# Query-key products of two heads, and the two low-rank products, issued in direct succession on the two row halves of the array

## The chip, the cores and the metric

The kernel runs on one core of one Trainium2 chip. The metric is device time in microseconds (us) of one execution. The kernel before takes 2220.48 us, the median of 3 runs (2214.12 to 2221.47). The engines are TensorE (PE in the profile; its weight loads are listed apart as PEld), VectorE (DVE), ScalarE (ACT), GpSimd (POOL) and SyncE (SP), which here issues most of the weight DMAs.

## The reference

Two transformer blocks over 512 tokens with model width 1024, in float32. The first block has a gated linear recurrence (hgrn2) beside a differential attention, and then a mixture of 32 experts, of which each token takes two. The second has an RWKV-7 mixer beside an attention over selected keys, a cross attention to 256 memory rows, and again 32 experts. Cut to what the change touches:

```python
def diff_attention(q1, q2, k1, k2, v, lam):      # 4 heads, q and k of 64, v of 128
    ...
        def probs(qb, kk):                       # a block of 128 queries
            s = jnp.einsum('bqhd,bshd->bhqs', qb, kk).astype(jnp.float32) * scale
            return jax.nn.softmax(jnp.where(mask, s, -jnp.inf), axis=-1)
        a = probs(qb1, k1) - lam * probs(qb2, k2)
        return jnp.einsum('bhqs,bshv->bqhv', a.astype(v.dtype), v)
...
    w = -jax.nn.softplus(-(w0 + jnp.tanh(xw) @ w2).astype(f32)) - 0.5     # rwkv7_branch, xw of 64
    decay = jnp.exp(-jnp.exp(w))
    a = jax.nn.sigmoid(a0 + xa @ a2)                                      # xa of 64
...
        s = jnp.einsum('bhqr,bqkr->bhqk', ql, c_sel).astype(f32)          # dsa_branch, 8 heads of 64
        s = jnp.where(valid[:, None], s, -jnp.inf)
        p = jax.nn.softmax(s, axis=-1).astype(c_sel.dtype)
```

All three have products that are contracted over 64 numbers, and there are always two of them that belong together: the two softmaxes of one head of the differential attention, the decay and the gate `a` of the low-rank products, and two of the eight heads of the selected attention.

## The kernel before

Activations lie in SBUF; the weights stream in. A dense layer multiplies a high and a low part of each operand (`split`, lines 193 to 196: ScalarE rounds the high part, VectorE subtracts it) in three products (`mm3`, line 198), each of which is an instruction of line 210 with a contraction over all 128 rows of the array. The other products are plain float32 and take two passes: one instruction leaves two matmul records in the trace.

A tensor whose two heads lie in partitions 0 to 63 and 64 to 127 gives two products over 64 rows each, one on the lower and one on the upper half of the array's rows. There are three such places:

- **Differential attention** (`dense1`, lines 541 to 573). For each of 4 heads and 4 blocks of 128 queries: for each of the two softmaxes the query-key product (line 551) into bank a0 or a1, the causal mask, added by a bf16 product (line 552), the maximum of the row (line 553, VectorE), the exponential with its sum (line 556, ScalarE). Then the two are combined on VectorE, transposed on TensorE (line 565) and copied; after four blocks the product with the values follows (line 569). A step with block i has n = 128, 256, 384 or 512 keys. The scheduler has the dense products of the same stage (banks d0 to d3) and those of the recurrence (lines 640 to 670) to put between.
- **Low-rank products** (`dense2`, lines 1295 to 1304). For each of 4 head pairs the decay's product (line 1298) and that of `a` (line 1302), each with a tanh on ScalarE behind it. Then VectorE has a scan and several products over 128 x 512.
- **Selected attention** (`dense2`, lines 1644 to 1676). For each of 4 head pairs p and 4 blocks i: the two query-key products (line 1655) into two of the three banks d0, d1 and a2 in turn, then per head the mask (line 1658), the row maximum (line 1660), a factor (line 1661), the exponential with its sum (line 1663), reciprocal and scaling (lines 1664 and 1665), i + 1 transposes (line 1668) and a copy (line 1669); then for both heads the products with the values (line 1674). After the fourth block the output of the pair is copied into `qT` (line 1676).

Behind the selected attention in the text stand products that do not depend on it: two gates and the RWKV branch's output projection, in the form `dense256` (lines 392 to 406, two banks a0 and a1). The attention's own output projection is the first thing to use `qT`: it is split on ScalarE and VectorE (`yb`, tile GG), and `dense` multiplies it (`ps_d<-GG,wh`).

The order of the work on each engine is not that of the text. A scheduler goes through the program with modelled times and puts ready instructions into each engine's queue, those of earlier lines first; `high_priority` raises a block. `keep_in_program_order` ties an instruction to its place in the text relative to the others that are so tied. On the chip an engine then works off its queue; semaphores make it wait for what it needs.

Of the kernel before, what the change touches and what calls it, by code (L numbers as in the profile page):

```python
# [29 lines left out]
AF = mybir.ActivationFunctionType  # L30
# [148 lines left out]
class Net:  # L179
# [28 lines left out]

    def mm(self, *a, **k):
        self.pin(self.nc.tensor.matmul(*a, **k))  # L210

    def persistent(self):
        tc, nc, es = self.tc, self.nc, self.es
# [195 lines left out]
    def dense1(self, rings, late):  # L409
        tc, nc, I = self.tc, self.nc, self.I  # L410
# [15 lines left out]
        o, n = self.at["cols2"]["norm_mem_2"]  # L426
        self.nmem = A.tile([128, 8], F32, name="nmem")
        nc.gpsimd.dma_start(self.nmem, I["cols2"][:, o:o + n])
        n = sum(v[1] for v in self.at["cols1"].values())
# [31 lines left out]
        o, n = self.at["cols1"]["hg_lb0"]  # L461
# [4 lines left out]
        for k in range(8):  # L466
            b = self.bank("a", (128, 256))
# [42 lines left out]
        qkT = big("C", (128, 2, 4, 512))  # L510
# [8 lines left out]
        for t in range(4):  # L519
            nv = raw[:, t, :].rearrange("p (i h d) -> p i h d", i=2, h=8)  # L520
            nc.vector.tensor_mul(nv, nv, rr[:, t][:, :, :, None].broadcast_to([128, 2, 8, 64]))
            a = k4([128, 2, 8, 64])
            bt = k4([128, 2, 8, 64])
            for i in range(2):
                nc.vector.tensor_mul(a[:, i], nv[:, i], cc[:, t, i][:, None, :].broadcast_to([128, 8, 64]))
                for s in range(2):
                    d0 = slice(s * 32, s * 32 + 32)
                    d1 = slice(32 - s * 32, 64 - s * 32)
# [3 lines left out]
            for i in range(2):  # L532
                b = self.bank("a")
# [6 lines left out]
        for h in range(4):  # L540
            vh = dv[:, :, h * 128:(h + 1) * 128]
            aT = B.tile([128, 4, 512], F32, name="aT", bufs=2)
            for i in range(4):
                n = (i + 1) * 128
                qs = slice(i * 128, n)
                st = wk.tile([128, 8], F32, name="da_st", bufs=4)
                ps = []
                for m in range(2):
                    r = slice(m * 64, (m + 1) * 64)
                    b = self.bank("a%d" % m)  # L550
                    nc.tensor.matmul(b[:, :n], qkT[r, 0, h, qs], qkT[r, 1, h, :n], start=True, stop=False)
                    nc.tensor.matmul(b[:, qs], idb, dgn, start=False, stop=True)
                    nc.vector.reduce_max(st[:, m:m + 1], b[:, :n], axis=AX.X)
                    nc.vector.tensor_scalar(st[:, 2 + m:3 + m], st[:, m:m + 1], -0.125, None, op0=ALU.mult)
                    pe = k3([128, 512])
                    nc.scalar.activation(pe[:, :n], b[:, :n], AF.Exp, scale=0.125, bias=st[:, 2 + m:3 + m],
                                         accum_out=st[:, 4 + m:5 + m])
                    ps.append(pe)
                nc.vector.reciprocal(st[:, 6:8], st[:, 4:6])
                nc.vector.tensor_scalar(ps[1][:, :n], ps[1][:, :n], st[:, 7:8], nlam, op0=ALU.mult, op1=ALU.mult)  # L560
                nc.vector.scalar_tensor_tensor(ps[0][:, :n], ps[0][:, :n], st[:, 6:7], ps[1][:, :n],
                                               op0=ALU.mult, op1=ALU.add)
                b = self.bank("a2")
                for j in range(i + 1):
                    nc.tensor.transpose(b[:, j * 128:(j + 1) * 128], ps[0][:, j * 128:(j + 1) * 128], ident)
                nc.scalar.activation(aT[:, :i + 1, qs], b[:, :n].rearrange("p (j q) -> p j q", q=128), AF.Copy)
            b = self.bank("a2")
            for j in range(4):
                nc.tensor.matmul(b[:, j * 128:], vh[:, j, :], aT[:, j, j * 128:], start=(j == 0), stop=(j == 3))
            nc.scalar.activation(vh, b.rearrange("p (j n) -> p j n", j=4), AF.Copy)  # L570
# [3 lines left out]
        r = A.tile([128, 4, 8], F32, name="onr", bufs=2)  # L574
        b = self.bank("a", (128, 4, 8))
# [6 lines left out]
        for h in range(4):  # L582
            b = self.tok_spread(r, 2 * h, 1)
            o = k3([128, 512])
# [5 lines left out]
        th = big("D")  # L590
# [47 lines left out]
        for m in range(4):  # L638
            tok = slice(m * 128, (m + 1) * 128)
            b = self.bank("a", (128, 4, 64))  # L640
# [6 lines left out]
            b = self.bank("a", (128, 4, 128))  # L647
# [4 lines left out]
            for p in range(2):  # L652
                r = slice(p * 64, (p + 1) * 64)
# [551 lines left out]
    def dense2(self):  # L1205
        tc, nc, I = self.tc, self.nc, self.I
# [9 lines left out]
        n = sum(v[1] for v in self.at["cols2"].values())  # L1216
# [15 lines left out]
        lora = big("lora", (128, 512))  # L1232
# [7 lines left out]
        omu, hw0, ha0, oka, hbg, hka = cc[:, 0:14], cc[:, 14:18], cc[:, 18:22], cc[:, 22:26], cc[:, 26:42], cc[:, 42:46]  # L1240
# [19 lines left out]
        xw = big("xw", (128, 512))  # L1260
# [33 lines left out]
        reset = self.reset(k3([128, 512]))  # L1294
        for p in range(4):
            pc = slice(p * 128, (p + 1) * 128)
            b = self.bank("a")
            nc.tensor.matmul(b, lora[0:64, pc], xw[0:64], start=True, stop=True)
            ld = tmp[:, p, 0]
            nc.scalar.activation(ld, b, AF.Tanh, scale=0.5, bias=hw0[:, p:p + 1])  # L1300
            b = self.bank("a")
            nc.tensor.matmul(b, lora[64:128, pc], xw[64:128], start=True, stop=True)
            th = tmp[:, p, 1]
            nc.scalar.activation(th, b, AF.Tanh, scale=0.5, bias=ha0[:, p:p + 1])
            nc.gpsimd.tensor_scalar(ld, ld, hc, hc, op0=ALU.mult, op1=ALU.add)
            cum = k2([128, 512])
            nc.vector.tensor_tensor_scan(cum, reset, ld, 0.0, op0=ALU.mult, op1=ALU.add)
            nc.vector.tensor_sub(ld, cum, ld)
            nc.scalar.activation(ld, ld, AF.Exp)
            nc.scalar.activation(AR[:, p, :, 1, :], v4(cum), AF.Exp)  # L1310
            nc.scalar.activation(cum, cum, AF.Exp, scale=-1.0)
            b = self.tok_spread(hs, 2 * p, 2)
            kkn = AR[:, p, :, 0, :]
            nc.vector.scalar_tensor_tensor(kkn, v4(kr[:, p, :]), col("rw_k_k_2")[:, p:p + 1], v4(b),
                                           op0=ALU.mult, op1=ALU.mult)
            nc.vector.scalar_tensor_tensor(bx[:, p], v5(th), 1.0, kkn.rearrange("p (m u) n -> p m u n", u=2),
                                           op0=ALU.add, op1=ALU.mult)
            nc.vector.scalar_tensor_tensor(kkn, kkn, -2.0, v4(ld), op0=ALU.mult, op1=ALU.mult)
            nc.gpsimd.tensor_mul(bx[:, p], bx[:, p], v5(cum))
            nc.vector.tensor_scalar(th, th, hka[:, p:p + 1], oka[:, p:p + 1], op0=ALU.mult, op1=ALU.add)  # L1320
            nc.vector.tensor_mul(kr[:, p, :], th, kr[:, p, :])
            nc.vector.tensor_mul(kx[:, p], v5(kr[:, p, :]), v5(cum))
# [51 lines left out]
        for p in range(4):  # L1374
            pc = slice(p * 128, (p + 1) * 128)
# [4 lines left out]
            b = self.bank("a", (128, 4, 128))  # L1380
# [265 lines left out]
        for p in range(4):  # L1646
            bo_ = self.bank("d3")
            for i in range(4):
                n = (i + 1) * 128
                qs = slice(i * 128, n)  # L1650
                sb = []
                for e in range(2):
                    r = slice(e * 64, e * 64 + 64)
                    b = self.bank(("d0", "d1", "a2")[(turn + e) % 3])
                    nc.tensor.matmul(b[:, :n], qT[r, p, qs], KT[r, p, :n], start=True, stop=False)
                    sb.append(b)
                for e, b in enumerate(sb):
                    nc.tensor.matmul(b[:, :n], idb, dgn if i == 0 else bias[:, bo[i]:bo[i] + n], start=False, stop=True)
                    st = wk.tile([128, 4], F32, name="st", bufs=4)
# [218 lines left out]
```

## Time and profile before

| | before |
|---|---|
| median of 3 runs | 2220.48 us |
| the profiled execution | 2217.94 us |
| its span, first to last instruction | 2216.1 us |
| mean granted TensorE clock | 0.976 |
| TensorE busy | 2134.3 us, 96% |
| TensorE's weight loads | 1376.3 us, 62% |
| VectorE busy | 989.7 us, 45% |
| ScalarE busy | 679.0 us, 31% |
| GpSimd busy | 161.1 us, 7% |

Shares are means over the whole span; stages differ. Loads overlap products on TensorE, so its two rows do not add up. Ends of products are modelled: where one starts before the one ahead has ended, the distance from start to start is what it costs. A granted clock of 1.00 is 2.4 GHz, 0.50 is 1.2 GHz.

### The profile page before, as it was taken

What the parts mean: (1) busy time and instruction counts of PE and PEld (TensorE: products, weight loads), DVE (VectorE), ACT (ScalarE), POOL (GpSimd) and SP (SyncE); (2) the same over time, 40 slices, a digit from 0 to 9 for tenths busy, and PEclk for the clock granted to TensorE, in tenths of its full rate; (3) what the DMA queues carried; (4) which work ended last, traced back from release to release, by engine and by line L of the source; (5) the groups of instructions that cost most, each with busy time, mean ns of one, the idle gap of its engine ahead of it and who ended that gap; (6) DMA issues with size and microseconds to landing.
All of it is one profiled execution on the core that took longest, in us unless ns stands there. A gap on an engine that the chain in (4) does not pass through costs nothing. (4 is left out here: it accounts for less than half of the span.)

```text
span 2216.1 us, 30270 instructions
## 1 busy us (share of the span) xinstructions
PE 2134.3 (96%) x12176; PEld 1376.3 (62%) x12176; DVE 989.7 (45%) x1998; ACT 679.0 (31%) x1313; POOL 161.1 (7%) x138
## 2 busy tenths in 40 slices
PE   8999999999999999998998999999898999999996
PEld 7766778785544744445766776667777544444443
DVE  4675323552323523334278485445455133333334
ACT  5364323232111321113533433443443211111113
POOL 0420001200000000000151100002110000000000
PEclk9999899999999999999998999999999999999998
DMA  4221121368999789994222112112624899999994
GB/s 176 84 67 48 48 105 66 141 275 342 401 419 420 300 341 418 420 420 145 84 67 75 60 45 86 38 58 86 254 77 172 338 377 418 419 419 420 420 420 165
DMA packets 95743, 505.89 MB, mean 228 GB/s; under 512 B 21024, under 2 KB 26144, under 8 KB 43888
## 3 DMA queue, kind: packets, MB, share of 16 engines
q1 hardware_dynamic: 90992, 490.09, 55.7%
q10 hardware_dynamic: 4112, 11.66, 1.4%
q8 instruction: 98, 1.61, 0.3%
q0 software_dynamic: 496, 2.17, 0.3%
q14 instruction: 45, 0.37, 0.1%
HBM read 494.83 MB, written 8.91 MB: 227 GB/s over the span
## 5 line engine op out<-in xcount | busy, mean ns | idle before, releaser
L210 PE MATMUL ps_d<-wslot,xg 128*64 128x512 f32 x2048 | 446.6, 593 | 2.4 <-DMA wslot<-in_wm_dram 2.4
L210 PE MATMUL ps_d<-hT,wh 128*128 128x512 f32 x1056 | 348.8, 415 | 2.5 <-DVE hT L301 2.5
L210 PEld LDWEIGHTS ps_d<-wslot,xg 128*64 128x64 f32 x2048 | 148.1, 137 | 289.0 <-issue 275.2
L196 DVE TENSOR_TENSOR wl<-wslot,wh 128x512 fp32r<-128x512 f32 x236 | 170.8, 729 | 286.1 <-ACT wh L195 233.7
L195 ACT ACTIVATE wh<-wslot 128x512 fp32r<-128x512 f32 x260 | 162.7, 630 | 321.9 <-PE ps_d L210 248.5
L210 PEld LDWEIGHTS ps_d<-hT,wh 128*128 128x128 f32 x1056 | 200.2, 196 | 55.6 <-issue 9.3
L210 PE MATMUL ps_d<-hT,wl 128*128 128x512 f32 x528 | 210.9, 411 | 0.5 <-DVE wl L196 0.5
L940 DVE TENSOR_TENSOR s<-ps_d,s 128x512 f32<-128x512 f32 x32 | 22.1, 692 | 420.7 <-PE ps_d L210 420.7
L210 PE MATMUL ps_a<-wslot,hidT 128*64 128x512 f32 (+1 forms) x800 | 173.1, 582 | 2.5 <-ACT hidT L948 2.1
L210 PE MATMUL ps_d<-wh,hT 128*128 128x512 f32 x512 | 165.4, 400 | 2.2 <-ACT wh L195 1.1
L978 DVE TENSOR_TENSOR acc<-acc,ps_a 128x512 f32<-128x512 f32 (+1 forms) x215 | 132.1, 667 | 50.7 <-PE ps_a L210 50.6
L210 PE MATMUL ps_a<-yy,S 128*128 128x512 f32 (+1 forms) x454 | 121.6, 397 | 8.7 <-DVE acc L978 5.6
L210 PEld LDWEIGHTS ps_a<-wslot,hidT 128*64 128x64 f32 x800 | 56.3, 137 | 106.4 <-issue 97.9
L210 PEld LDWEIGHTS ps_d<-hT,wl 128*128 128x128 f32 x528 | 103.0, 195 | 25.7 <-issue 1.9
L915 ACT ACTIVATE xg<-ps_a,gain 128x256 f32<-128x256 f32 x102 | 47.8, 475 | 220.2 <-PE ps_a L210 220.2
L210 PEld LDWEIGHTS ps_d<-wh,hT 128*128 128x128 f32 x512 | 96.3, 189 | 26.7 <-ACT wh L195 2.2
L210 PE MATMUL ps_a<-oh,xs 128*128 128x256 f32 x816 | 107.1, 285 | 2.9 <-DVE oh L1110 2.9
L210 PEld LDWEIGHTS ps_a<-oh,xs 128*128 128x128 f32 x816 | 100.3, 189 | 12.0 <-issue 12.0
L210 PE MATMUL ps_d<-wl,hT 128*128 128x512 f32 x256 | 102.6, 401 | 1.8 <-DVE wl L196 1.8
L210 PEld LDWEIGHTS ps_a<-yy,S 128*128 128x128 f32 x454 | 80.5, 191 | 33.9 <-DVE acc L978 13.9
L966 ACT ACTIVATE yy<-ps_a,gc 128x512 fp32r<-128x512 f32 (+1 forms) x50 | 33.6, 674 | 209.4 <-PE ps_a L210 185.8
L939 ACT ACTIVATE s<-ps_d 128x512 f32<-128x512 f32 x32 | 19.1, 598 | 199.6 <-PE ps_d L210 199.6
(615 smaller groups left out, 2886.5 us busy)
## 6 DMA issues: line engine op xcount, KB each, us to landing
wslot<-in_wm_dram SPq DMA_DIRECT2D x380, 1024.0 KB, 11.4
wslot<-in_wd_dram SPq DMA_DIRECT2D x108, 512.0 KB, 3.6
wslot<-in_wd_dram SPq DMA_DIRECT2D x19, 1024.0 KB, 12.2
wslot<-in_wm_dram SPq DMA_DIRECT2D x8, 512.0 KB, 13.8
C<-in_x_dram SPq DMA_DIRECT2D x4, 512.0 KB, 5.3
acc<-in_x_dram ACTq DMA_DIRECT2D x4, 512.0 KB, 5.2
kvd<-xg ACTq DMA_DIRECT2D x4, 512.0 KB, 3.6
xd<-acc ACTq DMA_DIRECT2D x1, 2048.0 KB, 11.8
```

What stands on the lines that cost most here:

```text
L195: self.nc.scalar.activation(hi, src, AF.Copy)
L196: (lo_eng or self.nc.vector).tensor_sub(lo, src, hi.bitcast(F32))
L210: self.pin(self.nc.tensor.matmul(*a, **k))
L915: nc.scalar.activation(xg[:, k, :n], b[:, :n], AF.Copy, scale=gain[:, k:k + 1])
L939: nc.scalar.activation(s1, hb[0], AF.Silu)
L940: nc.vector.tensor_mul(s1, hb[1], s1)
L966: nc.scalar.activation(y[0][:, c], b, AF.Copy, scale=gcol)
L978: nc.vector.tensor_add(acc[:, t, c], acc[:, t, c], b)
```

## The change

A helper issues the two products of a pair directly one behind the other, the second half (rows 64 to 127) first, and ties each to its program order. The masks and all that follows stay where they were in the text, behind both products. The banks are the same.

```diff
+    def side_by_side(self, xs, stop=True):
...
+        for o, l, r in xs[::-1]:
+            self.tc.keep_in_program_order(self.nc.tensor.matmul(o, l, r, start=True, stop=stop))
...
-                ps = []
-                for m in range(2):
-                    r = slice(m * 64, (m + 1) * 64)
-                    b = self.bank("a%d" % m)
-                    nc.tensor.matmul(b[:, :n], qkT[r, 0, h, qs], qkT[r, 1, h, :n], start=True, stop=False)
+                ps, sb = [], [self.bank("a%d" % m) for m in range(2)]
+                self.side_by_side([(sb[m][:, :n], qkT[m * 64:m * 64 + 64, 0, h, qs], qkT[m * 64:m * 64 + 64, 1, h, :n])
+                                   for m in range(2)], stop=False)
+                for m, b in enumerate(sb):
                     nc.tensor.matmul(b[:, qs], idb, dgn, start=False, stop=True)
...
-            b = self.bank("a")
-            nc.tensor.matmul(b, lora[0:64, pc], xw[0:64], start=True, stop=True)
+            wb = [self.bank("a") for _ in range(2)]
+            self.side_by_side([(wb[e], lora[e * 64:e * 64 + 64, pc], xw[e * 64:e * 64 + 64]) for e in range(2)])
             ld = tmp[:, p, 0]
-            nc.scalar.activation(ld, b, AF.Tanh, scale=0.5, bias=hw0[:, p:p + 1])
-            b = self.bank("a")
-            nc.tensor.matmul(b, lora[64:128, pc], xw[64:128], start=True, stop=True)
+            nc.scalar.activation(ld, wb[0], AF.Tanh, scale=0.5, bias=hw0[:, p:p + 1])
...
-                sb = []
-                for e in range(2):
-                    r = slice(e * 64, e * 64 + 64)
-                    b = self.bank(("d0", "d1", "a2")[(turn + e) % 3])
-                    nc.tensor.matmul(b[:, :n], qT[r, p, qs], KT[r, p, :n], start=True, stop=False)
-                    sb.append(b)
+                sb = [self.bank(("d0", "d1", "a2")[(turn + e) % 3]) for e in range(2)]
+                self.side_by_side([(sb[e][:, :n], qT[e * 64:e * 64 + 64, p, qs], KT[e * 64:e * 64 + 64, p, :n])
+                                   for e in range(2)], stop=False)
```

In the changed kernel all products of pairs are instructions of line 216; the lines of the differential attention move down by five, and those of the selected attention keep their numbers.

The order on TensorE in the differential attention, before. Tiles ps_a are the banks of the attention, ps_d those of the dense layer, C holds queries and keys, dgn and idb the mask's operands, cst the identity of the transposes; the number behind a name tells tiles of one name apart:

```order
L551 MATMUL ps_a_956<-C 128x512
L552 LDWEIGHTS idb
L552 MATMUL ps_a_956<-dgn,idb 128x128
L210 MATMUL ps_d_1537<-wl,hT_91 128x512
L210 MATMUL ps_d_1537<-wh,hT_92 128x512
L210 MATMUL ps_d_1538<-wh,hT_91 128x512
L551 MATMUL ps_a_963<-C 128x512
L565 MATMUL ps_a_928<-cst,k_916 128x128 x2
L552 LDWEIGHTS idb
L552 MATMUL ps_a_963<-dgn,idb 128x128
```

The same step on the same engine after, where the pair is one of line 216:

```order
L216 MATMUL ps_a_957<-C 128x512
L216 MATMUL ps_a_956<-C 128x512
L557 LDWEIGHTS idb
L557 MATMUL ps_a_956<-dgn,idb 128x128
L557 LDWEIGHTS idb
L557 MATMUL ps_a_957<-dgn,idb 128x128
L210 MATMUL ps_d_2031<-hT_91,wl 128x512
L210 MATMUL ps_d_2032<-hT_91,wh 128x512
```

Products of the two softmaxes had dense products and transposes between them; now they stand together, and both masks directly behind. Dense products follow up to the transposes.

The end of the selected attention on TensorE, before: the last step but one and the last (384 and 512 keys) of the last head pair. VU and qT hold keys and queries, X the mask, GG the transposed weights of the softmax, r and k the RWKV branch, wh and wl the weights:

```order
L1674 MATMUL ps_d_10795<-GG_10518,X_9172 64x128 x7
L1668 MATMUL ps_a_10957<-cst,k_10953 128x128
L1655 MATMUL ps_a_10996<-VU,qT 128x384
L1668 MATMUL ps_d_10974<-cst,k_10970 128x128 x2
L1658 LDWEIGHTS X_7724
L1658 MATMUL ps_a_10996<-X_7724 128x384
L1655 MATMUL ps_d_11030<-VU,qT 128x512
L1658 LDWEIGHTS X_7724
L1658 MATMUL ps_d_11030<-X_7724 128x512
L210 MATMUL ps_a_11360<-r,wh 128x512
L210 MATMUL ps_a_11360<-k,wh 128x512
```

The same place after:

```order
L1674 MATMUL ps_d_10933<-GG_10518,X_9172 64x128 x4
L216 MATMUL ps_a_10995<-VU,qT 128x384
L216 MATMUL ps_d_10994<-VU,qT 128x384
L1658 LDWEIGHTS X_7724
L1658 MATMUL ps_d_10994<-X_7724 128x384
L1658 LDWEIGHTS X_7724
L1658 MATMUL ps_a_10995<-X_7724 128x384
L1668 MATMUL ps_d_11006<-cst,k_11002 128x128 x3
L1668 MATMUL ps_a_11019<-cst,k_11015 128x128 x3
L1674 MATMUL ps_d_10933<-GG_10518,X_9172 64x128 x6
L216 MATMUL ps_d_11031<-VU,qT 128x512
L216 MATMUL ps_d_11030<-VU,qT 128x512
```

A step's products, masks, transposes and value products now stand one behind the other, and the pair of the next step behind the last of them; before, steps overlapped and dense products lay between.

Where that begins, and what follows the last step, on TensorE after. First the last dense products in the middle of the attention (second head pair, 256 keys):

```order
L210 MATMUL ps_a_11475<-r,wh 128x512
L210 MATMUL ps_a_11475<-k,wh 128x512
L210 MATMUL ps_a_11475<-r,wl 128x512
L1668 MATMUL ps_d_10698<-cst,k_10694 128x128 x2
L1668 MATMUL ps_a_10710<-cst,k_10706 128x128 x2
L1674 MATMUL ps_d_10657<-GG_10518,X_9172 64x128 x4
L216 MATMUL ps_d_10719<-VU,qT 128x384
L216 MATMUL ps_d_10718<-VU,qT 128x384
```

and then the end:

```order
L1674 MATMUL ps_d_10933<-GG_10518,X_9172 64x128 x8
L210 MATMUL ps_d_11523<-GG_11512,wh 128x512
L210 MATMUL ps_d_11524<-GG_11512,wh 128x512
L210 MATMUL ps_d_11525<-GG_11512,wh 128x512
L210 MATMUL ps_d_11526<-GG_11512,wh 128x512
```

Between these two places stand ten of the sixteen steps, without a dense product. Tile ps_a_11475 is the last of the work that does not depend on the attention; before, its products lay between the steps and behind the last of them.

## Rows read from the trace of the kernel before

**Rows 1.** The page's second part: the clock granted to TensorE in 40 equal slices of the span, in tenths of full speed.

```profile
PEclk9999899999999999999998999999999999999998
```

**Rows 2.** Stretches of the selected attention: from and to, us; its length, and busy us (instructions) of PE, PEld, DVE, ACT and POOL; the granted clock, the DMA's share and GB/s. The second line counts the instructions of line 210 alone (PE and PEld).

```profile
1368.20:1492.00 123.80, 123.80 (x610) 80.46 (x610) 55.42 (x163) 54.25 (x137) 0.00 (x0) 1.00 0.14 48
1368.20:1492.00 123.80, 69.76 (x272) 50.15 (x272) 1.00 0.14 48
```

**Rows 3.** TensorE's timeline in and behind the selected attention: start, us from the span's start; duration, us; engine, line, operation, output<-inputs, shapes, count of records.

```profile
1377.85 0.39 PE L210 MATMUL ps_a<-hT,wl 128*128 128x512 f32 x1
1378.17 0.70 PE L1655 MATMUL ps_d<-VU,qT 64*128 64x256 f32 x2
...
1447.32 0.48 PE L1655 MATMUL ps_d<-VU,qT 64*128 64x128 f32 x2
1447.73 0.23 PE L1658 MATMUL ps_d<-X 128*128 128x128 bf16 x1
...
1466.44 1.12 PE L1655 MATMUL ps_d<-VU,qT 64*128 64x512 f32 x2
1467.49 0.39 PE L1658 MATMUL ps_d<-X 128*128 128x512 bf16 x1
...
1491.99 1.31 PE L210 MATMUL ps_d<-GG,wh 128*128 128x512 f32 x5
```

**Rows 4.** TensorE's timeline in the index scores (tile pT), which are products over 64 rows, two heads at a time; columns as in rows 3.

```profile
1209.95 1.19 PE L210 MATMUL ps_a<-pT 64*128 64x256 f32 x4
1211.07 0.73 PE L210 MATMUL ps_d<-hT,wh 128*128 128x512 f32 x2
...
1212.66 0.70 PE L210 MATMUL ps_a<-pT 64*128 64x256 f32 x4
1213.29 0.50 PE L210 MATMUL ps_d<-hT,wh 128*128 128x512 f32 x1
...
1222.43 1.13 PE L210 MATMUL ps_a<-pT 64*128 64x512 f32 x4
1223.49 0.72 PE L210 MATMUL ps_d<-hT,wh 128*128 128x512 f32 x2
```

**Rows 5.** A stretch around the low-rank products; columns as in the first line of rows 2.

```profile
1110.00:1130.00 20.00, 20.00 (x79) 10.85 (x78) 18.39 (x22) 6.96 (x11) 10.44 (x6) 1.00 0.10 38
```

**Rows 6.** TensorE's timeline at the chunk products of the RWKV mixer; in brackets the idle time ahead of the row and what ended it.

```profile
1174.38 1.11 PE L1382 MATMUL ps_a<-cst,v 128*128 128x128 f32 x4 [3.93 <-DVE v L1252]
1175.14 1.20 PE L210 MATMUL ps_d<-hT,wh 128*128 128x512 f32 x2
```

**Rows 7.** The timelines of TensorE, VectorE and ScalarE in one step of the selected attention with 256 keys; columns as in rows 6.

```profile
1401.15 0.28 PE L1658 MATMUL ps_d<-X 128*128 128x256 bf16 x1
...
1402.38 0.47 ACT L1663 ACTIVATE k<-ps_d,st 128x256 f32<-128x256 f32 x1 [1.16 <-DVE st L1661]
...
1402.98 0.16 DVE L1664 RECIPROCAL st<-st 128x1 f32<-128x1 f32 x1 [0.56 <-ACT k L1663]
1403.18 0.35 DVE L1665 TENSOR_SCALAR k<-k,st 128x256 f32<-128x256 f32 x1
```

**Rows 8.** Groups of instructions by line and shape between 1365 and 1475 us: line, engine, operation, output<-input with their shapes, count | busy us, mean ns of one | idle us of the engine just before them, and what ended most of it.

```profile
L1660 DVE TENSOR_REDUCE st<-ps_d 128x1 f32<-128x512 f32 x6 | 4.2, 692 | 2.2 <-PE ps_d L1658 2.1
L1663 ACT ACTIVATE k<-ps_d,st 128x512 f32<-128x512 f32 x6 | 4.1, 683 | 0.6 <-DVE st L1661 0.6
L1665 DVE TENSOR_SCALAR k<-k,st 128x512 f32<-128x512 f32 x8 | 3.9, 485 | 0.3
...
L1669 ACT ACTIVATE GG<-ps_d 128x512 f32<-128x512 f32 x4 | 2.4, 598 | 2.1 <-PE ps_d L1668 2.0
...
L1665 DVE TENSOR_SCALAR k<-k,st 128x128 f32<-128x128 f32 x8 | 2.3, 285 | 0.2
L1663 ACT ACTIVATE k<-ps_d,st 128x128 f32<-128x128 f32 x6 | 2.2, 359 | 0.6 <-DVE st L1661 0.6
...
L1660 DVE TENSOR_REDUCE st<-ps_d 128x1 f32<-128x128 f32 x6 | 1.7, 285 | 1.7 <-PE ps_d L1658 1.7
```

**Rows 9.** TensorE's timeline in the selected attention, its transposes and value products; columns as in rows 3.

```profile
1446.73 0.66 PE L1668 MATMUL ps_d<-cst,k 128*128 128x128 f32 x4
...
1457.58 1.09 PE L1674 MATMUL ps_d<-GG,X 128*64 128x128 f32 x14
1458.60 0.33 PE L1668 MATMUL ps_a<-cst,k 128*128 128x128 f32 x1
```

**Rows 10.** ScalarE's timeline ahead of the attention's output projection: three of the four splits of `qT`.

```profile
1486.20 1.66 ACT L195 ACTIVATE GG<-qT 128x512 fp32r<-128x512 f32 x3
```

**Rows 11.** Stretches that show the granted clock; columns as in the first line of rows 2. The first two are the end of the recurrence of the first block, the next two the wait of rows 6 and what follows it, the last two the first and the last of four stretches at half clock in the differential attention.

```profile
343.80:347.20 3.40, 3.40 (x20) 2.72 (x19) 0.25 (x1) 0.22 (x1) 0.00 (x0) 1.00 0.47 153
347.20:350.60 3.40, 3.40 (x10) 2.61 (x9) 0.69 (x1) 2.36 (x5) 0.00 (x0) 0.50 0.00 1
1170.40:1174.40 4.00, 0.07 (x2) 0.03 (x1) 3.86 (x10) 0.00 (x0) 0.00 (x0) 0.85 0.07 25
1174.40:1180.00 5.60, 5.60 (x16) 4.54 (x17) 5.60 (x11) 1.19 (x2) 0.00 (x0) 0.50 0.22 76
220.90:227.70 6.80, 6.80 (x17) 4.68 (x18) 1.26 (x3) 1.10 (x4) 0.00 (x0) 0.50 0.00 0
275.50:278.90 3.40, 3.40 (x10) 2.61 (x9) 0.00 (x0) 2.86 (x4) 0.00 (x0) 0.50 0.33 114
```

More of the change, by code (lines that the diff above doesn't have):

```diff
@@ L1296, in dense2 @@
             pc = slice(p * 128, (p + 1) * 128)
-            b = self.bank("a")
-            nc.tensor.matmul(b, lora[0:64, pc], xw[0:64], start=True, stop=True)
+            wb = [self.bank("a") for _ in range(2)]
+            self.side_by_side([(wb[e], lora[e * 64:e * 64 + 64, pc], xw[e * 64:e * 64 + 64]) for e in range(2)])
             ld = tmp[:, p, 0]
-            nc.scalar.activation(ld, b, AF.Tanh, scale=0.5, bias=hw0[:, p:p + 1])
-            b = self.bank("a")
-            nc.tensor.matmul(b, lora[64:128, pc], xw[64:128], start=True, stop=True)
+            nc.scalar.activation(ld, wb[0], AF.Tanh, scale=0.5, bias=hw0[:, p:p + 1])
             th = tmp[:, p, 1]
-            nc.scalar.activation(th, b, AF.Tanh, scale=0.5, bias=ha0[:, p:p + 1])
+            nc.scalar.activation(th, wb[1], AF.Tanh, scale=0.5, bias=ha0[:, p:p + 1])
             nc.gpsimd.tensor_scalar(ld, ld, hc, hc, op0=ALU.mult, op1=ALU.add)
```

## Prediction

> **What bounds the kernel now.** I read the page first. TensorE is busy nearly throughout, and the clock granted to it is full nearly throughout: the slice line of the clock is to be read as nines with a few eights [rows 1]. So a saving on TensorE counts in full wherever its queue stays filled, and nothing that VectorE or ScalarE do matters unless TensorE has to wait for it. Next I took stretch tables of the places that the change touches. In the sparse attention, 1368.2 to 1492.0 us, TensorE is busy for all 123.8 us at full clock, while VectorE has 55 and ScalarE 54 us of work; 272 of TensorE's 610 matrix products there belong to dense layers (line 210) [rows 2]. The reader is to see that this stretch has no waits only because those 272 lie between the attention's steps. Last I read TensorE's timeline for the prices.
>
> **The change part by part.** *Price of a product alone.* A product of one head takes from its start to that of the mask product behind it 1447.32 to 1447.73 = 0.41 us at 128 keys and 1466.44 to 1467.49 = 1.05 at 512 [rows 3]; on the straight line between, 0.63 at 256 and 0.84 at 384.
>
> *Price of a pair in succession.* The trace has none of these pairs, but the index scores (64-row products, four records for two products) show three. Two of 256 columns last 1212.66 to 1213.29 = 0.63 us and two of 512 last 1222.43 to 1223.49 = 1.06: a pair at the price of one. The first group, 1209.95 to 1211.07, needs 1.12 for two of 256: no gain [rows 4]. A pair thus saves between nothing and one product; two of three groups say one product, which I take. A set of four widths saves 0.41 + 0.63 + 0.84 + 1.05 = 2.93 us. Beside it one change between 128-row and 64-row work is saved per step: a dense product ahead of a 64-row one takes 1377.85 to 1378.17 = 0.32 us where its usual spacing is (1.31 - 0.39) / 4 = 0.23 [rows 3], so 0.09 on the way in and about as much on the way out; I take 0.2 a step.
>
> *Differential attention* (4 heads, 16 steps): 4 x 2.93 + 16 x 0.2 = 14.9 us less. Between a pair and its transposes the new queue holds other work throughout; at 0.23 us a product that is more than the chain of a step as priced below, so I add no wait. *Low-rank products* (4 pairs of 512): 4 x 1.05 = 4.2 less on TensorE, but VectorE is busy 18.39 of 20 us there [rows 5], and part of it turns into waiting: between 0 and 5, I take 3.
>
> *Sparse attention* (16 steps). The pairs would save 4 x 2.93 + 3.2 = 14.9 us here too, but the order changes with it. In the old queue the transposes of one step, the products of the next and dense products are interleaved. In the new one each pair stands right behind the attention-value products (line 1674) of the step before, and the dense products run out at the transposes of the sixth step. For the last ten steps TensorE's queue is only: pair, two masks, transposes, attention-value products, next pair. TensorE takes its products in order: at 1174.38 it stood 3.93 us for VectorE's v, though the dense products queued behind, of 1175.14, were not waiting for v [rows 6].
> The Trainium skill ("TensorE: Matmul & The Clock Gate", Part 2) says so as a rule: only weight loads are pulled ahead, "The MATMULs themselves stay in program order". The trace agrees by those 3.93 us. If a waiting product could be passed, the chains of two steps would overlap, and the ten steps would be worth no more than their work on VectorE, some 25 us by the durations below instead of 57.
>
> So I price a bare step. At 256 keys, from the first mask product (1401.15) to the first exponential 1.23 us, one exponential with its accumulator until the reciprocal 0.60, the second the same 0.60, reciprocal 0.20, scaling 0.35 [rows 7]: 2.98 in all; I take 2.95, since the two masks need not be apart. Each 128 keys more add two reductions of (692 - 285) / 3 = 136 ns, two exponentials of 108 and one scaling of 67 [rows 8], 0.56 us, and I use 0.6 as bookkeeping of two heads costs too: 2.35, 2.95, 3.55, 4.15 for the four widths. TensorE's share is the pair (0.41, 0.63, 0.84, 1.05), the second head's transposes (0.33 to 0.66) and 2 to 8 attention-value products of (1458.60 - 1457.58) / 14 = 0.073 [rows 9], together 0.9, 1.4, 1.8 and 2.3. The copy (line 1669) is 0.60 at 512 [rows 8] and by the exponential's slope 0.28 at 128. With 0.2 for hand-offs a step takes 3.7, 4.9, 6.1 and 7.3 us. The ten steps are two full sets (2 x 22.0) and one of 384 and 512 (13.4): 57.4 us.
>
> The stretch before is 272 x 0.23 = 62.6 of dense products and 61.2 of attention, 15.3 a head pair. After: 62.6; six covered steps, one set less 3.7 (11.6) and the small half of another (4.4): 16.0; ten bare steps 57.4; and an end that was covered: the copy of the last output 0.6, then ScalarE's splits, four of its and one of weights, at 1.66 / 3 = 0.55 each [rows 10], 3.3. Sum 139.3, against 123.8: 15.5 us more, at full clock. So the gain of 14.9 is more than lost: the stretch sinks below the rate of TensorE because what hid the softmax has been used up.
>
> *The clock.* In the bare steps TensorE works about 17 of 57 us. After 1170.4 to 1174.4, in which it worked 0.07 of 4 us, the granted clock was 0.50 for the next 5.6 us; and even without idle time, after 343.8 to 347.2 with short products alone, it was 0.50 for 3.4 us [rows 11]. These are the two levels, 2.4 and 1.2 GHz. So I expect 0.5 in most of the bare steps. It costs between nothing and the doubling of TensorE's share, 2 x 6.4 + 1.8 + 2.3 = 16.9 us; I take 14, as parts of a step (weight loads, hand-offs) need not double. Afterwards the dense layer starts at half clock: by the 5.6 us above 2.8 lost at most, I take 2.5. Together 16.5.
>
> Sum against the profiled execution's 2217.94 us (2.5 under the median of the runs): - 14.9 - 3 + 15.5 + 16.5 = + 14.1, so 2232 us. The DMA queues keep their order, and no transfer is late here.
>
> **The rivals.** (1) *The clock stays full in the bare steps.* For it: most of the kernel runs at full clock [rows 1]; against it, the two falls of rows 11. Without the 16.5 it is 2232 - 16.5 = 2215.5 us: no change. (2) *Faster: the closer succession keeps the clock up in the differential attention too.* Four stretches between 220.9 and 278.9, 20.5 us together, ran at 0.50, the first and the last are in rows 11; at full clock they would take half, 10 less. With the bare steps also at full clock this gives 2215.5 - 10 = 2206 us. It decides once the bare steps, their clock included, take less than 63 us, and at 57 once over four of the ten are regained. Against it: these stretches too are ones in which short products of the recurrence, not waits, stand ahead. (3) *The pairs do not run side by side*, as the first group of rows 4: the 11.7 + 11.7 + 3 are lost, the bare steps stay, 2259 us.
>
> **How the numbers follow.** Forecast 0.67, rival (1) 0.18, (2) 0.10, (3) 0.05. The forecast's own range is 2222 to 2246 (the clock's price 6 to 20, hand-offs 0.1 to 0.6 a step, and up to 8 us of waits in the differential attention if its cover is thinner than I think). The whole range takes in rival (1) and leaves out (2) and (3): 2212 to 2246. A measurement of this kernel cannot tell less than 0.3%, 6.7 us, from no change. Slower by more: nearly all of the forecast and (3), 0.68. Within: (1), and the forecast's lower edge, 0.22. Faster: (2), 0.10. The break-even of the change is a mean bare step of about 6 us, clock included; I price 7.1.
>
> **What would show it right or wrong.** Right: rows of line 216 with four records, 0.63 us long at 256 and 1.06 at 512; the differential attention about 15 us shorter; then at the end of the sparse attention a stretch of 60 to 75 us in which TensorE is below half busy, its idle time ended by VectorE's scaling (line 1665) and ScalarE's copy (line 1669), with a granted clock near 0.5, and a wait of about 3 us for the splits ahead of the last dense layer. Wrong: if these ten steps take less than 6 us in the mean, if the clock stays at 1.0 in them, or if the pairs of line 216 last as long as two products. TensorE's busy time elsewhere must stay as it was; a difference there would mean that the order moved at a place that I did not price.

## The result: slower by half a per cent, and the profile after

The changed kernel takes 2225.18 us in the median of 10 runs (2218.67 to 2233.51), the kernel before 2212.59 in 10 runs; the ratio is 1.0053, with a 95% interval of 1.0037 to 1.0069. That is 12.6 us more, where the prediction had 14.1. The profiled execution of the changed kernel took 2226.69 us, 8.75 more than that of before, which lies 5 us above the median of its ten. Ratios and means over runs leave out those in a slower state, one of the kernel before at 2247.39 us and one of the sixth experiment at 2408.54. Its page begins so, and the clock line answers to [rows 1]:

```profile
span 2224.9 us, 30267 instructions
...
PE 2111.4 (95%) x12176; PEld 1372.4 (62%) x12176; DVE 989.6 (44%) x1998; ACT 678.2 (30%) x1313; POOL 160.5 (7%) x138
...
PEclk9999999999999999998999999869999999999998
```

TensorE has the same 12176 product records and is busy 23 us less (2134.3 before), yet the span is 9 us longer: its time was saved in one place and turned into waiting in another. Where, the clock line shows at once: slices 26 and 27, with an 8 and a 6, are the end of the selected attention.

Stretch tables of the stages of both executions follow, with columns as in [rows 2]; first the kernel before: the stage of the differential attention (from its first transposed queries to the last part of the mixed output), the mixture of experts behind it, and the stage of the low-rank products up to the index scores.

```profile
88.30:429.40 341.10, 339.91 (x1548) 255.54 (x1546) 162.92 (x304) 136.94 (x269) 37.52 (x32) 0.95 0.20 67
473.50:1037.50 564.00, 542.54 (x3188) 293.73 (x3185) 203.74 (x439) 122.18 (x225) 4.76 (x3) 0.99 0.87 354
1037.50:1210.80 173.30, 160.38 (x1140) 120.85 (x1140) 110.18 (x185) 70.44 (x116) 52.48 (x38) 0.91 0.28 93
```

The same three of the changed kernel, and then its selected attention, the first line of which answers to [rows 2]; of the three behind it the first is the part ahead of the ten steps without dense products, the second these ten steps, and the third the time from their end to beyond the first products of the next layer:

```profile
87.20:408.40 321.20, 320.38 (x1543) 248.65 (x1542) 159.97 (x304) 136.70 (x269) 39.26 (x31) 0.97 0.21 72
452.50:1012.40 559.90, 539.28 (x3188) 290.52 (x3186) 203.82 (x439) 122.11 (x225) 4.75 (x3) 0.99 0.87 357
1012.40:1189.30 176.90, 156.46 (x1139) 121.10 (x1140) 111.96 (x185) 69.24 (x115) 49.55 (x38) 0.91 0.28 91
...
1346.70:1498.90 152.20, 126.81 (x609) 85.52 (x608) 55.65 (x162) 53.96 (x135) 0.00 (x0) 0.83 0.13 42
1346.70:1424.65 77.95, 77.58 (x387) 58.85 (x386) 33.66 (x81) 30.76 (x70) 0.00 (x0) 1.00 0.24 78
1424.65:1497.75 73.10, 49.23 (x223) 26.68 (x222) 22.00 (x80) 22.05 (x62) 0.00 (x0) 0.66 0.01 4
1497.75:1501.00 3.25, 2.08 (x5) 1.70 (x6) 2.10 (x4) 2.67 (x5) 0.00 (x0) 0.50 0.00 0
```

The differential attention is 20 us shorter, the experts 4 (nothing was changed there), the low-rank stage is 4 longer, and the selected attention (the sparse one of the prediction), from the end of the last product of line 1642 (1645 in the changed kernel) to the start of the first of its output projection, takes 152.2 us where it took 123.9 (1368.1 to 1492.0), 28 more. Its VectorE and ScalarE have the work they had; TensorE is busy for 126.8 of 152.2 us. Up to 1424.65 TensorE hardly waits and its clock is 1.00; what is lost is lost behind it, in 1424.65 to 1497.75, where the clock is 0.66, and in 1.2 us of waiting after that.

The fifth of the ten steps on TensorE, with 384 keys, and the beginning of the sixth; columns as in [rows 6]:

```profile
1452.44 1.01 PE L216 MATMUL ps_d<-VU,qT 64*128 64x384 f32 x1
1452.45 1.01 PE L216 MATMUL ps_a<-VU,qT 64*128 64x384 f32 x1
1453.24 0.84 PE L216 MATMUL ps_d<-VU,qT 64*128 64x384 f32 x1
1453.25 0.84 PE L216 MATMUL ps_a<-VU,qT 64*128 64x384 f32 x1
1454.03 0.50 PE L1658 MATMUL ps_a<-X 128*128 128x384 bf16 x1
1454.32 0.52 PE L1658 MATMUL ps_d<-X 128*128 128x384 bf16 x1
1457.21 0.87 PE L1668 MATMUL ps_d<-cst,k 128*128 128x128 f32 x3 [2.37 <-DVE st L1664]
1457.88 0.85 PE L1668 MATMUL ps_a<-cst,k 128*128 128x128 f32 x3
1458.67 2.18 PE L1674 MATMUL ps_d<-GG,X 128*64 128x128 f32 x12
1460.78 1.22 PE L216 MATMUL ps_a<-VU,qT 64*128 64x512 f32 x1
```

From one pair to the next it takes 1460.78 - 1452.44 = 8.3 us. TensorE stands 2.37 us for the softmax, and what it does itself is slow: this pair needs 1.59 us to the mask. The same pair earlier in the attention, where dense products lay between and the clock was full, needs 1375.66 - 1374.81 = 0.85:

```profile
1374.81 0.59 PE L216 MATMUL ps_a<-VU,qT 64*128 64x384 f32 x1
1374.82 0.59 PE L216 MATMUL ps_d<-VU,qT 64*128 64x384 f32 x1
1375.24 0.48 PE L216 MATMUL ps_a<-VU,qT 64*128 64x384 f32 x1
1375.24 0.48 PE L216 MATMUL ps_d<-VU,qT 64*128 64x384 f32 x1
1375.66 0.34 PE L1658 MATMUL ps_d<-X 128*128 128x384 bf16 x1
...
1388.50 1.13 PE L216 MATMUL ps_d<-VU,qT 64*128 64x512 f32 x4
1389.56 0.61 PE L1658 MATMUL ps_d<-X 128*128 128x512 bf16 x2
```

So the pair itself does what it should: both first passes start within 10 ns of each other, both second passes too, and two products of 384 keys cost 0.85 us, two of 512 cost 1.06, the price of one in [rows 3]. All 36 pairs of the changed kernel start 6 or 7 ns apart.

TensorE's waits from 1424.65 to 1501 in the changed kernel: line that waited, what for, us in total, times, longest.

```profile
PE ps_d L1668 <- DVE st L1664: 19.4, 8, 2.9
PE ps_d L1668 <- DVE k L1665: 3.9, 2, 1.9
PE ps_d L210 <- ACT GG L195: 1.2, 1, 1.2
```

Ten waits of the transposes for the softmax, 23.3 us, one a step; the kernel before has none of these.

### The profile page after: what moved, and what is told of

Read it like the earlier page. It is cut to its first block, busy times and chain, and to the rows that moved or that the text cites. A ratio compares the mean times of both kernels' runs of the same rounds, so it can differ in the third digit from the quotient of the medians.

```text
span 2224.9 us, 30267 instructions
## 1 busy us (share of the span) xinstructions
PE 2111.4 (95%) x12176; PEld 1372.4 (62%) x12176; DVE 989.6 (44%) x1998; ACT 678.2 (30%) x1313; POOL 160.5 (7%) x138
```

## The experiments

The theory to be tested (A): the two products side by side are worth what the prediction says, and the loss comes from the tie of the first product of a pair. `keep_in_program_order` was told ahead of the prediction as an order among instructions that are so tied. It does more: it puts an instruction behind the one that stands ahead of it in the text on its engine, tied or not, as the order of the first experiment shows. For the first product of a step that is the last value product of the step before. Hence the single file that the order shows. The rival (B) is that the pair itself does it, since it needs two of the three banks at once. C and D are about the clock, E about the differential attention.

**1. The tie without the pair.** The kernel before with one tie:

```diff
-                    nc.tensor.matmul(b[:, :n], qT[r, p, qs], KT[r, p, :n], start=True, stop=False)
+                    mm = nc.tensor.matmul(b[:, :n], qT[r, p, qs], KT[r, p, :n], start=True, stop=False)
+                    if e == 0:
+                        self.tc.keep_in_program_order(mm)
```

> The kernel before, in which only the first of the two query-key products of a step of the selected attention is tied to its place in the text, behind the value products of the step before; the products are not put together, and the rest is as before. Theory A (the tie of the first product, not the pair, puts the steps in single file, so that the dense products run out after six steps): the selected attention takes 30 to 40 us longer than before, ten steps at the end stand without dense products at a mean of 7 us or more, and the ratio to before is 1.013 to 1.019. Theory B (what costs is that the pair needs two banks at once and issues both heads together): nothing of that, ratio 0.998 to 1.002.

Measured: 2258.77 us, ratio 1.021 (1.0178 to 1.0242), even more than A had. The stretch of the selected attention:

```profile
1365.10:1532.60 167.50, 144.97 (x606) 92.98 (x609) 55.50 (x162) 53.74 (x135) 0.00 (x0) 0.78 0.11 38
```

It is 43.6 us longer than before with no pair in it. So the tie alone is enough for the loss, and B falls. Its single file is not quite that of the changed kernel: the free second product of the next step stands ahead of the transposes, and nine times TensorE waits with it until an exponential (line 1665 of this kernel) is done.

```profile
PE ps_d L1655 <- ACT k L1665: 10.1, 6, 2.3
PE ps_a L1655 <- ACT k L1665: 5.8, 3, 2.3
```

So the difference to the changed kernel, 167.5 - 152.2 = 15.3 us, is no measure of the pairs, close as it is to the 14.9 that the prediction had for them.

**2. Only the second product tied.** The changed kernel, at all three places:

```diff
-        for o, l, r in xs[::-1]:
-            self.tc.keep_in_program_order(self.nc.tensor.matmul(o, l, r, start=True, stop=stop))
+        for k, (o, l, r) in enumerate(xs[::-1]):
+            i = self.nc.tensor.matmul(o, l, r, start=True, stop=stop)
+            if k:
+                self.tc.keep_in_program_order(i)
```

> The changed kernel with only the second product of each pair tied, behind the first; the first may go as soon as it is ready. Theory A: the steps of the selected attention overlap again, the stretch takes 108 to 120 us where before took 124 and the changed kernel 154; with 13 to 21 us less in the differential attention the ratio to before is 0.985 to 0.992. Theory B: the stretch stays over 140 us, ratio 1.000 to 1.006.

Measured: 2188.15 us, ratio 0.9889 (0.9865 to 0.9913), faster than both kernels. The stretch:

```profile
1347.50:1460.40 112.90, 109.39 (x607) 75.37 (x609) 55.36 (x162) 52.35 (x135) 0.00 (x0) 0.98 0.17 57
```

11 us less than before, not the 14.9 of the pairs. TensorE is idle for 3.5 us of it, which before had none; the last step stands without cover in this order too. Its order has 15 of the 16 pairs side by side and dense products between the steps up to the last. Around one pair:

```profile
1386.99 1.09 PE L1676 MATMUL ps_d<-GG,X 128*64 128x128 f32 x14
1388.01 0.33 PE L1670 MATMUL ps_a<-cst,k 128*128 128x128 f32 x1
1388.27 0.92 PE L216 MATMUL ps_d<-VU,qT 64*128 64x384 f32 x4
1389.11 0.44 PE L1670 MATMUL ps_d<-cst,k 128*128 128x128 f32 x2
1389.38 0.49 PE L1660 MATMUL ps_d<-X 128*128 128x384 bf16 x2
1389.58 0.76 PE L210 MATMUL ps_a<-hT,wh 128*128 128x512 f32 x2
```

The transposes of the step before (line 1670 of this kernel) stand behind the pair here, so steps overlap again, and dense products follow. The first product is free to go early, and the second nearly always stands at once behind it; one pair of the attention and three of the four low-rank ones were pulled apart all the same.

**3. The selected attention as before.** The changed kernel with the old lines at the third place:

```diff
-                sb = [self.bank(("d0", "d1", "a2")[(turn + e) % 3]) for e in range(2)]
-                self.side_by_side([(sb[e][:, :n], qT[e * 64:e * 64 + 64, p, qs], KT[e * 64:e * 64 + 64, p, :n])
-                                   for e in range(2)], stop=False)
+                sb = []
+                for e in range(2):
+                    r = slice(e * 64, e * 64 + 64)
+                    b = self.bank(("d0", "d1", "a2")[(turn + e) % 3])
+                    nc.tensor.matmul(b[:, :n], qT[r, p, qs], KT[r, p, :n], start=True, stop=False)
+                    sb.append(b)
```

> The changed kernel with the selected attention as before; the pairs of the differential attention and of the low-rank products stay. Theory A: the whole loss lies in the selected attention, the stretch there takes 124 us again, and what is left is a gain of 15 to 24 us, ratio 0.989 to 0.993. If the loss of 5 us that the changed kernel shows ahead of the low-rank products (the lead over the kernel before falls from 25 to 20 us there) belongs to these pairs and not to one execution, the lead falls by 5 us at this place here too.

Measured: 2195.24 us, ratio 0.9928 (0.9903 to 0.9952), and the stretch is that of before again:

```profile
1346.20:1470.10 123.90, 123.74 (x606) 80.44 (x609) 55.44 (x163) 54.28 (x137) 0.00 (x0) 1.00 0.14 47
```

So two places gain 0.7% and the third gives back more than that. The dip ahead of the low-rank products came again: the lead over the kernel before fell from 25.5 us at the end of the experts to 20.6 at the first projections of the second block. But the first experiment, which has the queue of before up to the selected attention, shows it as well, 11.1 to 6.8, and the fourth, with the changed kernel's code there, does not (21.1 to 21.3). It is a difference between executions and does not belong to the pairs. Part of it is the clock, which was at half there for 6.8 us more than before in the third experiment and for 3.4 us more in the first.

**4. The waits filled.** The changed kernel with extra products whose results are overwritten (`tb[0]` is the bank of the transposes):

```diff
+                tb = [self.bank(("d2", "a3")[e]) for e in range(2)]
+                if 4 * p + i >= 6:
+                    for x in range((6, 8, 9, 11)[i]):
+                        self.tc.keep_in_program_order(nc.tensor.matmul(
+                            tb[0], hT[0][:, x % 8, 0:128], hT[0][:, x % 8, :], start=True, stop=True))
+                for e, b in enumerate(sb):
...
-                    b = self.bank(("d2", "a3")[turn % 2])
+                    b = tb[turn % 2]
```

> The changed kernel with 6, 8, 9 or 11 extra dense products (128 x 512, their results are overwritten by the transposes) behind the masks of each of the last ten steps of the selected attention, where TensorE waits for the softmax. Theory C (half the clock in these steps costs 14 us of TensorE's own share): TensorE is never idle for long, the clock stays at 1.0, and the ten steps take 57 to 63 us instead of 73 although there is more work; ratio to before 0.996 to 1.001. Theory D (the clock costs nothing there, the chain through VectorE and ScalarE is what takes 7.3 us a step): the ten steps take 73 us or more, ratio 1.004 or more.

Measured: 2211.63 us, ratio 0.9998 (0.9982 to 1.0014): 2 x 34 + 20 = 88 more products, and faster than the changed kernel by 0.55%. The stretch of its ten steps:

```profile
1424.13:1483.68 59.55, 53.78 (x308) 33.50 (x310) 22.00 (x80) 22.08 (x62) 0.00 (x0) 1.00 0.01 5
```

TensorE's waits for the scaling in them:

```profile
PE ps_d L1674 <- DVE k L1671: 2.8, 10, 0.4
```

The ten steps take 59.55 us at a clock of 1.00 instead of 73.10 at 0.66, and TensorE still waits ten times, once a step, for the scaling (line 1671 of this kernel), so the extra products are not what sets a step's length. C holds: half the clock costs 13.5 us here. What is left is the chain itself, 59.55 us.

**5. The order of the differential attention without the pair.** The kernel before with the four instructions of a step together and tied, but a mask between the products:

```diff
...
-                    nc.tensor.matmul(b[:, :n], qkT[r, 0, h, qs], qkT[r, 1, h, :n], start=True, stop=False)
-                    nc.tensor.matmul(b[:, qs], idb, dgn, start=False, stop=True)
+                    self.tc.keep_in_program_order(
+                        nc.tensor.matmul(b[:, :n], qkT[r, 0, h, qs], qkT[r, 1, h, :n], start=True, stop=False))
+                    self.tc.keep_in_program_order(nc.tensor.matmul(b[:, qs], idb, dgn, start=False, stop=True))
+                    sb.append(b)
+                for m, b in enumerate(sb):
```

> The kernel before, in which the differential attention issues product, mask, product, mask of a step together and ties all four to their place in the text: its steps stand in the new order, but the two products, with a mask between, cannot run side by side. Theory A (the gain there comes from two products at the price of one): no gain, ratio 0.998 to 1.002. Theory E (it comes from the order, by a steadier clock and fewer changes between dense and short products): most of the 12 to 15 us come back, ratio 0.993 to 0.996.

Measured: 2219.67 us, ratio 1.0038 (1.0024 to 1.0052): no gain, so E falls, but a loss of some 8 us that A did not have either. One step of its order:

```profile
195.53 1.12 PE L552 MATMUL ps_a<-C 64*128 64x512 f32 x2
196.58 0.23 PE L553 MATMUL ps_a<-dgn,idb 128*128 128x128 bf16 x1
196.74 1.12 PE L552 MATMUL ps_a<-C 64*128 64x512 f32 x2
```

Its stage of the differential attention:

```profile
86.80:422.30 335.50, 334.76 (x1545) 255.48 (x1544) 164.44 (x304) 137.58 (x269) 37.89 (x32) 0.97 0.20 69
```

To compare such stages, their clock has to be taken out, as executions of one and the same queue differ in it. The first and the sixth experiment both have the queue of before there. The stage in the first:

```profile
86.70:420.70 334.00, 332.82 (x1545) 251.01 (x1543) 163.03 (x304) 136.57 (x269) 37.00 (x31) 0.97 0.21 69
```

and in the sixth:

```profile
86.80:427.20 340.40, 339.25 (x1545) 255.36 (x1543) 163.04 (x304) 136.77 (x269) 37.04 (x32) 0.95 0.20 68
```

Length times clock is 324.0 and 323.4 us, for the profile of before 341.1 x 0.95 = 324.0, for this kernel 325.4, and for the changed one 321.2 x 0.97 = 311.6. The clock has two digits, so each may be off by 1.7. The stretches at half clock in the traces, added up, are finer: 30.7 us in the profile of before, 17.1 in the first experiment, 30.7 in the sixth, 20.5 here and 20.5 in the changed kernel. With half of that taken off, the lengths are 325.7, 325.5, 325.0, 325.3 and 311.0. So the pairs are worth some 14 us here, and the new order without them nothing. The 8 us that this kernel loses are not in this stage of its profile, and most of them go with the clock: over its 12 runs the mean was 0.977, over the 28 of before 0.980, and the mean span times clock is 2166.3 us against 2164.7. Why the clock was lower is open.

**6. The low-rank pairs alone.** The kernel before with the changed kernel's lines at the second place:

```diff
...
+            wb = [self.bank("a") for _ in range(2)]
+            self.side_by_side([(wb[e], lora[e * 64:e * 64 + 64, pc], xw[e * 64:e * 64 + 64]) for e in range(2)])
...
```

> The kernel before with the pairs of the low-rank products alone. Theory A (VectorE is the bound there, so the 4 us saved on TensorE turn into waiting): 0 to 2 us less, ratio 0.9985 to 1.001. Rival: the full 4 us or more, ratio 0.996 to 0.998.

Measured: 2212.54 us, ratio 1.0 (0.9983 to 1.0017). The pairs run at the price of one here too (in the changed kernel one lasts from 1103.46 to 1104.52 us). What comes of it is not told: the interval takes in nothing and also 3 us less (0.9986); the full 4.2 us lie just outside. The mean span times clock is 3.1 us less than before's (2161.6 against 2164.7), at a mean clock of 0.978 against 0.980, so the pairs may have saved their 3 us and the clock taken them back.

**7. No tie at all.** The changed kernel with plain products, one behind the other in the text:

```diff
-            self.tc.keep_in_program_order(self.nc.tensor.matmul(o, l, r, start=True, stop=stop))
+            self.nc.tensor.matmul(o, l, r, start=True, stop=stop)
```

> The changed kernel without any tie: the two products of a pair stand one behind the other in the text only. Theory A (the scheduler then pulls them apart again, to the order of before in the selected attention): ratio 0.996 to 1.002, the stretch of the selected attention 124 us. Rival (adjacent text is enough): as with the second product tied, ratio 0.985 to 0.992.

Measured: 2204.4 us, ratio 0.9978 (0.9962 to 0.9994). In the selected attention the scheduler returned to the order of before, and the stretch was 123.9 us. In the differential attention two of the sixteen pairs stayed together. Its stage reads

```profile
86.70:415.70 329.00, 328.30 (x1543) 248.63 (x1542) 162.41 (x304) 136.90 (x269) 38.35 (x32) 0.98 0.21 71
```

of which 13.7 us were at half clock; with half of that taken off it is 322.2 us, 3 less than the kernels without pairs and 11 more than the changed one. So a neighbour in the text is seldom one in the queue, and the gain of the pairs needs a tie. The 0.2% that this kernel gains go mostly with the clock: over its runs the mean was 0.982, over those of before 0.980, and the mean span times clock is 2163.3 us against 2164.7.

**8. Both tied at the first two places, the second alone at the third.**

```diff
...
+            if k or first:
+                self.tc.keep_in_program_order(i)
...
+                                   for e in range(2)], stop=False, first=False)
```

> Both products of a pair tied in the differential attention and the low-rank products, as in the changed kernel, and only the second in the selected attention. Theory A: the gains of the second and the third experiment add up where they are different places: ratio 0.986 to 0.991, no slower than the version with the second product tied everywhere.

Measured: 2190.11 us, ratio 0.9903 (0.988 to 0.9926). This is not told apart from the second experiment, whose interval overlaps it. So the tie of the first product shows no cost at the first two places; it costs at the third, where the work between the steps runs out.

## Why the prediction was right

The direction, the time and the main mechanism were right: 14.1 us more forecast, 12.6 more measured in the medians and 8.75 in the profiled executions (2232 us forecast, 2226.69 measured). By its steps:

- **Price of a pair.** Taken: two products at the price of one, 0.41 to 1.05 us. Measured 0.85 at 384 keys and 1.06 at 512. Rival (3) fell (its sum is 2258 us, not 2259), and with it the first group of [rows 4] as a pattern. The trace of before has six such groups, not three, and in five of them the two products start within 10 ns of each other; in the first they start 0.49 us apart at a clock of 1.00, in the changed kernel too. Why is open.
- **Differential attention, 14.9 less.** Measured 20 in the profile; with the time at half clock taken out some 14. The rest is the clock of the one execution of before (0.95 against 0.97), not the change. No wait was added, as forecast. Rival (2), a steadier clock there, has no support: stages of one queue had 0.95 and 0.97.
- **Low-rank products, 3 less.** Not told apart from nothing: the ratio of these pairs alone is 1.0, and its interval takes in 3 us less. That VectorE, busy 18.39 of 20 us [rows 5], eats part of the saving was tested by no run.
- **Selected attention.** The covered part from the first mark to the first bare step was put at 62.6 + 16.0 = 78.6 us; it took 1424.65 - 1346.70 = 77.95. The ten bare steps were put at 57.4 at full clock, and 59.55 were measured where the clock was kept full; with half the clock 57.4 + 14 = 71.4, measured 73.1. The price of the clock was 14, measured 13.5. At full clock the four widths took 3.9, 5.0, 6.3 and 7.6 us where 3.7, 4.9, 6.1 and 7.3 were priced. That this is so close is in part luck: 0.073 us is the price of one record [rows 9], and a value product leaves two (12 for the six products of 384 keys above), so the prediction has half their time, 3.9 us too little over the ten steps; its other terms together were some 2 us too large.
- **The end, 3.3.** This term was too large: 1.2 us of waiting were measured, because TensorE can begin with the first of the four splits, and I let it wait for all. ScalarE's timeline at that place:

```profile
1497.75 0.60 ACT L1676 ACTIVATE qT<-ps_d 128x512 f32<-128x512 f32 x1 [1.80 <-PE ps_d L1674]
1498.24 2.18 ACT L195 ACTIVATE GG<-qT 128x512 fp32r<-128x512 f32 x4
```

and TensorE's:

```profile
1498.92 2.50 PE L210 MATMUL ps_d<-GG,wh 128*128 128x512 f32 x5 [1.20 <-ACT GG L195]
```

- **The restart at half clock, 2.5.** The five products above take 2.50 us where five took 1.31 [rows 3], and the changed kernel's lag behind the kernel before grew from 6.9 us at the first of them to 8.95 ten products later, where it stayed, so 2.0.
- **Added up.** Measured, with the time at half clock in the differential attention taken out: - 14 + 28.3 + 2.0 = 16.3 us more. The 4 us from there to the 12.6 of the medians were not placed; the low-rank pairs may be 3 of them.

Two of the signs of being right did not show. TensorE was to be below half busy in the bare steps and was busy 49.23 of 73.10 us: the 17 us that the prediction gave it leave out the masks, the first head's transposes and half of the value products. And the clock was to be near 0.5 and was 0.66, at half for two thirds of the time. The idle time was ended by VectorE as forecast (reciprocal or scaling, lines 1664 and 1665, 23.3 us), by the copy of line 1669 for 0.2 us only.

Rival (1), a full clock in the bare steps, was told apart by the fourth experiment: it would have been no change, and with the waits filled it was (0.9998). What the prediction did not have is the cause of the single file. It read the new order and priced it rightly, but did not say which part of the change made it. It is the tie of the first product and not the pair; with that tie alone the kernel is slower by 2.1%, and without it the same pairs make it faster by 1.1%.

The rule of the Trainium skill ("TensorE: Matmul & The Clock Gate", Part 2) that products stay in program order agrees with these runs: ten times the transposes stood for the softmax, 23.3 us together, and the next pair behind them started only after them. It does not by itself make the single file: what stands in the queue behind a waiting product decides what the wait costs, and the second experiment shows how much another order gets back.

## What to carry to other kernels

Here two products on the two row halves of the array cost one in all pairs of the changed kernel, with nothing between them in the queue (the first group of [rows 4] is a case where they did not), and this is worth having where TensorE is the bound. But where the work between steps is scarce, a tie that makes them neighbours should bind the second to the first and not the first to what is ahead of it: otherwise steps that overlapped go in single file, and the work that hid their softmax is used up early. Before a change to the order is timed, count how many steps have filling work between their product and the use of its result; each step without it costs the length of its chain, and again something for the clock.

## What the runs showed of the hardware

- The two products of a pair start within 10 ns of each other, pass by pass, and this for float32 products of two passes each, into two different banks.
- Work whose results are thrown away made a kernel faster: 88 dense products in the waits of ten steps kept the granted clock at 1.00 and took 13.5 us off these steps.
- Executions of one queue differ in granted clock: in the differential attention's stage 0.97 in one and 0.95 in two, 334.0, 340.4 and 341.1 us. A difference of some 7 us there is no sign of a change.
- With one wait of 1.7 to 2.9 us in each of ten steps the mean granted clock was 0.66; with these waits filled by 88 more products it was 1.00.
